# A decoder trunk on one core: the order of one attention unit, with the value products a unit later

## The chip, the core and the metric

The kernel runs on one core of a Trainium2 chip. TensorE (PE, with its weight loads PEld) multiplies matrices into PSUM banks, VectorE (DVE), ScalarE (ACT) and GpSimd (POOL) work on vectors, and SyncE (SP) issues transfers. The engines run side by side and wait for one another by semaphores. Each engine works through its own instructions in the order in which it is given them, so an instruction that waits holds back everything queued behind it on the same engine. The metric is the device time of one execution in microseconds, the median of several.

## The reference

One decoder layer on 2048 positions of width 1024, in float32. What the change touches is the attention: 16 query heads and 2 key/value heads of width 64, in blocks of 128 queries that see their own block and the one before, with a bias by distance and a sink in each head's softmax.

```
u = x * (1 + scale) + shift
[q | k | v | attn_gate | pool_in | pool_gate | merge_a | merge_p] = u @ W_in
logits = (q . k) / 8 + bias, masked to the last 128 positions
probs  = softmax([logits, sink])[..., :-1]
a = (probs @ v) * SiLU(attn_gate) @ W_attn_proj
p = GroupLinear(MultiScaleCausalPool(pool_in)) * pool_scale * SiLU(pool_gate) @ W_pool_proj
x = LayerNorm(alpha * x + ((sigmoid(merge_a) * a + sigmoid(merge_p) * p) @ W_out) * (1 + gate))
```

## The kernel before

A float32 product is made from pieces: an operand x is split into a high part that TensorE takes exactly and a low part, x minus high, and three matmuls (high by high, high by low, low by high) are added up in PSUM. Splitting a tile is so always a copy on one engine (mostly ScalarE) and a subtraction on another (`low`, line 132, mostly VectorE).

The 2048 positions are worked through in two halves. Each half has a ring of gate products (with the products for query tiles 0 and 1 in it, each tile holding the queries of two heads) and then an attention phase, `attention` (line 736). After both come the output products and the layer norm. The large weight products use a block scheme with fewer multiplications; its additions run on GpSimd.

`attention` has one loop, `for n in range(N + 5)` (line 925), over units. A unit n is one query tile j (two heads) and one block of 128 queries; a half has N = 64 of them, eight for each of eight tiles. The loop is a pipeline written out by hand. In one iteration it works on several units:

- S(n): `score_mms` (line 828), four matmuls of queries by keys into a bank `lg` (two buffers).
- the score step on VectorE, one instruction a head: bias added, and the row's bound `nm` reduced, into the tile L; then ScalarE's exponential with the row's sum `sm`. A small ScalarE copy puts the sink into L before.
- for unit n-1, the reciprocal of `sm` (line 937, VectorE), the scaling of the first head's row (ScalarE) and of the second head's (VectorE, called E1 in the prediction).
- T(n-2): `turn_mms` (line 842), four transposes of the scaled weights into the bank `pt` (one buffer); then ScalarE copies the high part `pth` (line 958), and VectorE subtracts for the low part `ptl`. Each of these has one buffer.
- V: `value_mms` (line 849), four matmuls of the values with `pth` and `ptl` into the bank `pv` (one buffer). The values carry their high and low parts side by side, so the result's two halves have to be added: ScalarE copies one half into `o2` (line 946), and VectorE adds it to the other into the output tile `o`, one instruction a head ("the additions").
- `project(n)` (line 873): nine or twelve matmuls of the next query tiles and of the pool branch, which keep TensorE busy while the other engines do the softmax; from unit 60 on `fill_one` (line 912) does the first products of the next phase in their place.

At the unit's end come steps that are due only in some units: `take_q` (line 757) splits a finished query tile (two ScalarE, then two VectorE instructions), `pool_sums` and `pool_diff` (lines 775 and 792) make the pool branch (ScalarE copies, GpSimd sums, one VectorE subtraction), `finish` (line 804) multiplies by gates on GpSimd and queues stores, and weight tiles are fetched and split.

The order on ScalarE, VectorE, TensorE and GpSimd is the order of the text: `act`, `dve`, `pe` and `pool` are wrapped in `Ordered` (line 50), which keeps each engine's instructions as written. Calls through `nc.` are placed by the planner.

Of the kernel before, what the change touches and what calls it, by code (L numbers as in the profile page):

```python
# [12 lines left out]
F32 = mybir.dt.float32  # L13
F32R = mybir.dt.float32r
AF = mybir.ActivationFunctionType
# [4 lines left out]
P = 128  # L20
# [3 lines left out]
CH = 512  # L24
# [35 lines left out]
def kernel(  # L60
# [675 lines left out]
    def attention(ph, s, q0, nxt):  # L736
# [91 lines left out]
        def score_mms(j, b, q, qs):  # L828
            k0 = P if s == 0 and b == 0 else 0
            lg = bank("lg").rearrange("p (h k) -> p h k", h=2)  # L830
            for h in range(2):
                for hl in range(2):
                    mm(
                        lg[:, h, k0:],
                        qs[:, h, q * P : (q + 1) * P],
                        kk[:, j // 4, hl, b * P + k0 : (b + 2) * P],
                        start=hl == 0,
                        stop=hl == 1,
                    )
# [46 lines left out]
        bts = {0: bias_tile(0)}  # L886
        raw_q = {}
        parts, accs, sums = {}, {}, {}
        lgs, exps, Ls, pvs, outs, ags, pgs = {}, {}, {}, {}, {}, {}, {}
        opened = []  # L890
        act.activation(warm, mhalf, AF.Exp)

# [32 lines left out]
        for n in range(N + 5):  # L925
            j, t, b = n // U, n // NB % 2, n % NB
            if n == 0:
                project(n)
            if n < N:
                lgs[n] = score_mms(j, n % U, b, qs[j, t])  # L930
            pt = None
            if n - 2 in Ls:
                L, k0 = Ls.pop(n - 2)
                pt = turn_mms(L, k0)
            if n - 1 in exps:
                sm = exps[n - 1][2]
                dve.reciprocal(sm, sm)
            if n - 3 in pvs:
                pv = pvs.pop(n - 3)
                jj, tt, bb = (n - 3) // U, (n - 3) // NB % 2, (n - 3) % NB  # L940
                if bb == 0:
                    outs[jj, tt] = tp.tile([P, CH], F32, tag="o", bufs=2, name="o")
                if bb == 1:
                    ags[jj, tt] = ld("ag", gates_d["ag"][s, jj, tt])
                o2 = tp.tile([HD, 2, P], F32, tag="o2", bufs=2, name="o2")
                act.copy(o2, pv[HD:])
                for h in range(2):
                    dve.tensor_tensor(
                        outs[jj, tt][h * HD : (h + 1) * HD, bb * P : (bb + 1) * P], pv[0:HD, h, :], o2[:, h, :], ALU.add
                    )  # L950
            if n - 1 in exps:
                E, e0, sm = exps[n - 1]
                act.activation(E[:, 0, e0:256], E[:, 0, e0:256], AF.Copy, scale=sm[:, 0:1])
            if pt is not None:
                h0 = k0 // P
                pth = tp.tile([P, 2, 2, P], F32R, tag="pth", bufs=1, name="pth")
                ptl = tp.tile([P, 2, 2, P], F32R, tag="ptl", bufs=1, name="ptl")
                act.copy(pth[:, h0:], pt[:, h0:])
            if n < N:
                lg, c0 = lgs.pop(n)  # L960
                L = tp.tile([P, 2, 260], F32, tag="L", bufs=3, name="L")
                nm = tp.tile([P, 2], F32, tag="nm", bufs=4, name="nm")
                sm = tp.tile([P, 2], F32, tag="sm", bufs=4, name="sm")
                act.copy(L[:, :, 256], nsink[:, 2 * j : 2 * j + 2])
# [19 lines left out]
                exps[n] = (L, c0, sm)  # L984
            if pt is not None:
                low(dve, ptl[:, h0:], pt[:, h0:], pth[:, h0:])
            if n - 1 in exps:
                E, e0, sm = exps.pop(n - 1)
                dve.tensor_scalar(E[:, 1, e0:256], E[:, 1, e0:256], sm[:, 1:2], None, ALU.mult)
                Ls[n - 1] = (E, e0)  # L990
            if 0 < n < 60:
                project(n)
            elif n >= 60:
                fill_one(n)
            if pt is not None:
                pvs[n - 2] = value_mms((n - 2) // U, (n - 2) % U, k0, pth, ptl)


            for w in range(1, len(order)):
                at = first[2 * w - 2]  # L1000
                if n == at:
                    tiles[w] = fetch(*order[w])
                if n in (at + 1, at + 2) and tiles[w][0] is not None:
                    raw, hi, lo = tiles[w]
                    if n == at + 1:
                        act.copy(by_two(hi), raw)
                    else:
# [12 lines left out]
            for what in puts:  # L1020
                put(pool if n >= 64 else sp, *what)
            puts.clear()
            for at, x, which in ((57, 0, 0), (60, 1, 0), (62, 0, 1), (64, 1, 1)):
                if n == at:
                    early_hi(x, which)
                if n == at + 1:
                    early_lo(x, which)
            if n in (59, 62):
                nxt_group[n // 62].mid()
            if n == 64:  # L1030
                opened[0].append(nxt_group[0].w[:, 0, :])
                act.copy(opened[0][4], opened[0][0])
            for x, at in done.items():
                kind, m, st = x
                if kind == "q":
                    continue
                if n == at + 2:
                    pgs[m, st] = ld("pg", gates_d["pg"][s, m, st])
                if n == at + 3 + (st == 1 and m + 1 < KT):
                    pl = pool_diff(m, sums.pop((m, st)), accs.pop(x))  # L1040
                    finish("p", pin_d[s], m, st, pl, pgs.pop((m, st)))
            for x, at in done.items():
                if x[0] == "mix" and n == at + 1:
                    sums[x[1:]] = pool_sums(*x[1:], accs[x])
            for x in [x for x in outs if n == x[0] * U + x[1] * NB + NB + 2]:
                finish("a", ain_d[s], *x, outs.pop(x), ags.pop(x))

            if n in (26, 42):
                fill_set("T1", n // 42, nxt_store["T1"], sp)
            for start, name in ((57, "B11"), (58, "B21"), (59, "T2"), (61, "B22")):  # L1050
                if n == start:
                    for half in range(2):
                        fill_set(name, half, nxt_store[name], sp)
            if n == 51:
                for q in nxt_group:
                    q.load(ph, False)
# [488 lines left out]
```

## Time and profile before

| | |
|---|---|
| median of 3 runs | 1769.96 us (1766.4 to 1770.78) |
| the profiled execution | 1771.75 us |
| its span, first to last instruction | 1769.9 us |
| mean granted TensorE clock | 0.992 |
| first attention stretch | 427 to about 690 us |
| second attention stretch | about 1030 to 1298 us |

In the rows that follow, a line of the timeline is: start, length, engine, source line, operation, written tile <- read tiles, shapes, count, and in brackets the idle time of that engine before it and what ended it. Nearly every row names line 56, which is the wrapper that keeps the order, so rows are told apart by the tiles. A row of waits is: who waited for whom, total us, times, longest. `pv` is the value bank, `lg` the score bank, `pt` the bank of the turned weights, `mm` a projection bank, `L` the weights of a unit, `sm` their sums.

### The profile page before, as it was taken

To read this page: it belongs to the slowest core of one execution; us is meant where nothing else is said; L and a number is where in the kernel's file an instruction comes from. 1 tells how busy PE (TensorE), PEld (TensorE's weight loads), DVE (VectorE), ACT (ScalarE), POOL (GpSimd) and SP (SyncE) were. 2 spreads that over 40 slices of the span, in tenths; PEclk is the share of its full clock that TensorE was granted. 3 is DMA by queue.
4 is the path that set the end of the run, shared out by engine and by line. 5 is a ranking of instruction groups with operands and counts; after the bars stand their busy time and mean duration, and the time that the engine had idled before them with its cause. 6 is when DMAs were issued, how large, how long until landed. Compare 5 with 4: busy or idle time off the path is not lost. (4 is left out here: it accounts for less than half of the span.)

```text
span 1769.9 us, 24992 instructions
## 1 busy us (share of the span) xinstructions
PE 1701.8 (96%) x8224; PEld 1422.5 (80%) x8224; DVE 1212.4 (68%) x2188; ACT 941.5 (53%) x1983; POOL 803.5 (45%) x624
## 2 busy tenths in 40 slices
PE   6899999999999998999999999999999989999997
PEld 5688888888888887888788888888878767888785
DVE  5977656546777777767745457777867676865777
ACT  4644444436777776444444367777744333423452
POOL 2155444530545567433424224455763663363542
PEclk9999999999999999999999999999999999999998
DMA  9385767853434467687776544454696684699432
GB/s 364 119 287 178 266 215 262 286 130 125 167 135 166 147 230 301 242 276 262 260 273 230 188 162 163 141 178 136 246 355 221 191 261 170 240 322 366 155 143 107
DMA packets 182161, 383.40 MB, mean 217 GB/s; under 512 B 18944, under 2 KB 39440, under 8 KB 182032
## 3 DMA queue, kind: packets, MB, share of 16 engines
q1 hardware_dynamic: 175392, 366.02, 59.1%
q0 software_dynamic: 3552, 11.56, 1.7%
q10 hardware_dynamic: 3088, 4.23, 0.9%
q8 instruction: 65, 1.06, 0.2%
q14 instruction: 64, 0.52, 0.1%
HBM read 245.40 MB, written 139.49 MB: 217 GB/s over the span
## 5 line engine op out<-in xcount | busy, mean ns | idle before, releaser
L56 PE MATMUL mm<-set_B,w_set 128*128 128x512 f32 x3096 | 768.5, 395 | 12.4 <-DVE w_set L133 5.5
L56 PEld LDWEIGHTS mm<-set_B,w_set 128*128 128x128 f32 x3096 | 577.3, 189 | 134.2 <-DVE w_set L133 10.6
L56 PE MATMUL lg<-set_T,w_set 128*128 128x512 f32 x2160 | 523.6, 392 | 17.3 <-DVE w_set L133 9.3
L56 PEld LDWEIGHTS lg<-set_T,w_set 128*128 128x128 f32 x2160 | 404.2, 188 | 110.8 <-DVE w_set L133 14.9
L133 DVE TENSOR_TENSOR w_set<-W,w_set 128x1024 fp32r<-128x1024 f32 x168 | 232.2, 1382 | 205.4 <-ACT w_set L326 195.2
L326 ACT CAST w_set<-W 128x1024 fp32r<-128x1024 f32 x168 | 176.3, 1050 | 266.8 <-PE mm L56 204.9
L56 PE MATMUL mm<-set_T,w_set 128*128 128x512 f32 x1032 | 257.6, 394 | 0.0
L56 PEld LDWEIGHTS mm<-set_T,w_set 128*128 128x128 f32 x1032 | 192.3, 189 | 39.5
L295 POOL TENSOR_TENSOR W<-W,A 128x512 f32<-128x512 f32 x58 | 86.5, 1491 | 237.9 <-DMA A<-in_win_dram 58.2
L304 POOL TENSOR_TENSOR W<-W 128x512 f32<-128x512 f32 x58 | 81.8, 1410 | 189.0 <-DVE w_set L133 178.7
L56 ACT ACTIVATE L<-L,nm 128x257 f32<-128x257 f32 (+1 forms) x256 | 127.1, 498 | 11.0 <-DVE nm L56 5.7
L299 POOL TENSOR_TENSOR W<-W 128x512 f32<-128x512 f32 x58 | 92.0, 1587 | 89.5 <-DVE w_set L133 80.4
L56 DVE TENSOR_TENSOR o<-pv,o 64x128 f32<-64x128 f32 x256 | 72.4, 283 | 81.0 <-ACT o L56 77.9
L56 DVE CUSTOM_DVE_ANT_0 L<-lg,bt,nsink 128x256 f32<-128x256 f32 (+1 forms) x256 | 111.6, 473 | 5.7 <-PE lg L56 1.7
L300 POOL TENSOR_TENSOR W<-W 128x512 f32<-128x512 f32 x58 | 94.6, 1630 | 43.8 <-DMA W<-in_win_dram 27.6
L56 POOL TENSOR_TENSOR p<-nxt,pg 128x512 f32<-128x512 f32 x32 | 41.3, 1292 | 113.5 <-DVE sm L56 113.0
L56 POOL TENSOR_TENSOR nxt<-vb 128x512 f32<-128x512 f32 (+3 forms) x32 | 34.2, 1068 | 122.7 <-ACT vb L56 122.7
L56 DVE TENSOR_TENSOR ptl<-pt,pth 128x512 fp32r<-128x512 f32 (+1 forms) x128 | 85.6, 669 | 1.7 <-ACT pth L56 1.5
L56 ACT COPY o<-pv 64x256 f32<-64x256 f32 x128 | 47.3, 370 | 66.1 <-PE pv L56 65.0
L56 DVE TENSOR_TENSOR k_lo<-spare,k_hi 128x512 fp32r<-128x512 f32 x61 | 61.4, 1009 | 30.0 <-ACT k_hi L56 13.2
L56 ACT ACTIVATE L<-L,sm 128x256 f32<-128x256 f32 (+1 forms) x128 | 64.3, 502 | 31.6 <-DVE sm L56 31.6
L56 PE MATMUL lg<-kk,qs 128*128 128x256 f32 (+1 forms) x512 | 80.3, 279 | 0.0
(217 smaller groups left out, 2347.3 us busy)
## 6 DMA issues: line engine op xcount, KB each, us to landing
W<-in_win_dram SPq DMA_DIRECT2D x48, 512.0 KB, 4.9
w_set<-wmix_d SPq DMA_DIRECT2D x28, 512.0 KB, 4.7
W<-in_win_dram SPq DMA_DIRECT2D x36, 256.0 KB, 3.2
A<-in_win_dram SPq DMA_DIRECT2D x36, 256.0 KB, 4.5
ag_d<-sig SPq DMA_DIRECT2D x32, 256.0 KB, 3.5
pg_d<-sig SPq DMA_DIRECT2D x32, 256.0 KB, 3.5
ma_d<-sig SPq DMA_DIRECT2D x32, 256.0 KB, 4.0
mp_d<-sig SPq DMA_DIRECT2D x32, 256.0 KB, 3.7
```

The costliest lines, as they stand in the source:

```text
L56: return lambda *args, **kw: self.tc.keep_in_program_order(op(*args, **kw))
L133: engine.tensor_tensor(dst, src, as32(hi), ALU.subtract)
L295: e.tensor_tensor(self.w[:, 1, :], self.w[:, 2, :], self.a22, ALU.add)
L299: e.tensor_tensor(x[:, 1, :], x[:, 1, :], x[:, 0, :], ALU.subtract)
L300: e.tensor_tensor(x[:, 2, :], x[:, 0, :], x[:, 2, :], ALU.subtract)
L304: e.tensor_tensor(x[:, 3, :], x[:, 3, :], x[:, 1, :], ALU.subtract)
L326: a.copy(by_two(hi), raw)
```

## The change

In the same loop, the order of an iteration changes and the value products come a unit later, for unit n-3 in place of n-2. What each engine does in iteration n, in order:

| engine | before | after |
|---|---|---|
| TensorE | S(n), T(n-2), projection, V(n-2) | S(n), V(n-3), T(n-2), projection |
| ScalarE | o2(n-3), first head's scaling(n-1), pth(n-2), sink copy(n), exponentials(n) | sink copy(n), first head's scaling(n-1), o2(n-3), pth(n-2), exponentials(n) |
| VectorE | reciprocal(n-1), additions(n-3), score steps(n), ptl(n-2), second head's scaling(n-1) | reciprocal(n-1), score steps(n), ptl(n-2), second head's scaling(n-1), additions(n-3) |

The steps that are due only in some units still follow all this. The tile `o` and the load of the gate `ag` move with the additions. No buffer count changes. The core of the diff:

```diff
             if n < N:
-                lgs[n] = score_mms(j, n % U, b, qs[j, t])
-            pt = None
+                lg, c0 = score_mms(j, n % U, b, qs[j, t])
+            pt = pv = None
+            if n - 3 in turned:
+                pv = value_mms((n - 3) // U, (n - 3) % U, *turned.pop(n - 3))
             if n - 2 in Ls:
                 L, k0 = Ls.pop(n - 2)
-                pt = turn_mms(L, k0)
+                pt, h0 = turn_mms(L, k0), k0 // P
+            if 0 < n < 60:
+                project(n)
+            elif n >= 60:
+                fill_one(n)
+            if n < N:
+                L = tp.tile([P, 2, 260], F32, tag="L", bufs=3, name="L")
...
+                act.copy(L[:, :, 256], nsink[:, 2 * j : 2 * j + 2])
             if n - 1 in exps:
-                sm = exps[n - 1][2]
-                dve.reciprocal(sm, sm)
-            if n - 3 in pvs:
-                pv = pvs.pop(n - 3)
...
+                E, e0, r = exps[n - 1]
+                dve.reciprocal(r, r)
+                act.activation(E[:, 0, e0:256], E[:, 0, e0:256], AF.Copy, scale=r[:, 0:1])
+            if pv is not None:
                 o2 = tp.tile([HD, 2, P], F32, tag="o2", bufs=2, name="o2")
                 act.copy(o2, pv[HD:])
-                for h in range(2):
-                    dve.tensor_tensor(
-                        outs[jj, tt][h * HD : (h + 1) * HD, bb * P : (bb + 1) * P], pv[0:HD, h, :], o2[:, h, :], ALU.add
-                    )
...
             if pt is not None:
                 low(dve, ptl[:, h0:], pt[:, h0:], pth[:, h0:])
+                turned[n - 2] = k0, pth, ptl
             if n - 1 in exps:
-                E, e0, sm = exps.pop(n - 1)
-                dve.tensor_scalar(E[:, 1, e0:256], E[:, 1, e0:256], sm[:, 1:2], None, ALU.mult)
+                E, e0, r = exps.pop(n - 1)
+                dve.tensor_scalar(E[:, 1, e0:256], E[:, 1, e0:256], r[:, 1:2], None, ALU.mult)
                 Ls[n - 1] = (E, e0)
-            if 0 < n < 60:
-                project(n)
-            elif n >= 60:
-                fill_one(n)
-            if pt is not None:
-                pvs[n - 2] = value_mms((n - 2) // U, (n - 2) % U, k0, pth, ptl)
+            if pv is not None:
...
+                for h in range(2):
+                    dve.tensor_tensor(
+                        outs[jj, tt][h * HD : (h + 1) * HD, bb * P : (bb + 1) * P], pv[0:HD, h, :], o2[:, h, :], ALU.add
+                    )
```

More of the change, by code (lines that the diff above doesn't have):

```diff
@@ L888, in attention @@
         parts, accs, sums = {}, {}, {}
-        lgs, exps, Ls, pvs, outs, ags, pgs = {}, {}, {}, {}, {}, {}, {}
+        exps, Ls, turned, outs, ags, pgs = {}, {}, {}, {}, {}, {}
         opened = []
@@ L929, in attention @@
             if n < N:
-                lgs[n] = score_mms(j, n % U, b, qs[j, t])
-            pt = None
+                lg, c0 = score_mms(j, n % U, b, qs[j, t])
+            pt = pv = None
+            if n - 3 in turned:
+                pv = value_mms((n - 3) // U, (n - 3) % U, *turned.pop(n - 3))
             if n - 2 in Ls:
                 L, k0 = Ls.pop(n - 2)
-                pt = turn_mms(L, k0)
-            if n - 1 in exps:
-                sm = exps[n - 1][2]
-                dve.reciprocal(sm, sm)
-            if n - 3 in pvs:
-                pv = pvs.pop(n - 3)
[L940 to L944, printed above, removed]
+                pt, h0 = turn_mms(L, k0), k0 // P
[5 more added lines that the diff above has]
+                L = tp.tile([P, 2, 260], F32, tag="L", bufs=3, name="L")
+                nm = tp.tile([P, 2], F32, tag="nm", bufs=4, name="nm")
+                sm = tp.tile([P, 2], F32, tag="sm", bufs=4, name="sm")
+                act.copy(L[:, :, 256], nsink[:, 2 * j : 2 * j + 2])
+            if n - 1 in exps:
+                E, e0, r = exps[n - 1]
+                dve.reciprocal(r, r)
+                act.activation(E[:, 0, e0:256], E[:, 0, e0:256], AF.Copy, scale=r[:, 0:1])
+            if pv is not None:
                 o2 = tp.tile([HD, 2, P], F32, tag="o2", bufs=2, name="o2")
                 act.copy(o2, pv[HD:])
-                for h in range(2):
-                    dve.tensor_tensor(
-                        outs[jj, tt][h * HD : (h + 1) * HD, bb * P : (bb + 1) * P], pv[0:HD, h, :], o2[:, h, :], ALU.add
-                    )
-            if n - 1 in exps:
-                E, e0, sm = exps[n - 1]
-                act.activation(E[:, 0, e0:256], E[:, 0, e0:256], AF.Copy, scale=sm[:, 0:1])
             if pt is not None:
-                h0 = k0 // P
                 pth = tp.tile([P, 2, 2, P], F32R, tag="pth", bufs=1, name="pth")
@@ L959, in attention @@
             if n < N:
[L960 to L964, printed above, removed]
                 for h in range(2):
@@ L986, in attention @@
                 low(dve, ptl[:, h0:], pt[:, h0:], pth[:, h0:])
+                turned[n - 2] = k0, pth, ptl
             if n - 1 in exps:
-                E, e0, sm = exps.pop(n - 1)
-                dve.tensor_scalar(E[:, 1, e0:256], E[:, 1, e0:256], sm[:, 1:2], None, ALU.mult)
+                E, e0, r = exps.pop(n - 1)
+                dve.tensor_scalar(E[:, 1, e0:256], E[:, 1, e0:256], r[:, 1:2], None, ALU.mult)
                 Ls[n - 1] = (E, e0)
-            if 0 < n < 60:
-                project(n)
-            elif n >= 60:
-                fill_one(n)
-            if pt is not None:
-                pvs[n - 2] = value_mms((n - 2) // U, (n - 2) % U, k0, pth, ptl)
+            if pv is not None:
+                jj, tt, bb = (n - 3) // U, (n - 3) // NB % 2, (n - 3) % NB
+                if bb == 0:
+                    outs[jj, tt] = tp.tile([P, CH], F32, tag="o", bufs=2, name="o")
+                if bb == 1:
+                    ags[jj, tt] = ld("ag", gates_d["ag"][s, jj, tt])
+                for h in range(2):
+                    dve.tensor_tensor(
+                        outs[jj, tt][h * HD : (h + 1) * HD, bb * P : (bb + 1) * P], pv[0:HD, h, :], o2[:, h, :], ALU.add
+                    )
             for w in range(1, len(order)):
```

## The prediction

> **What bounds the kernel now.** I read the page first (engine shares), then the busy time by stretch, then the waits of TensorE's weight loads inside the two attention stretches, then the order of time in two units of the loop.
>
> ```profile
> span 1769.9 us, 24992 instructions
> PE 1701.8 (96%) x8224; PEld 1422.5 (80%) x8224; DVE 1212.4 (68%) x2188; ACT 941.5 (53%) x1983; POOL 803.5 (45%) x624
> ```
>
> The busy time by stretch (PE, PEld, DVE, ACT, POOL, then granted clock, DMA share and GB/s), first and second attention stretch:
>
> ```profile
> 427.00:720.00 293.00, 283.62 (x1570) 243.15 (x1569) 219.26 (x652) 214.86 (x625) 162.40 (x135) 0.99 0.53 188
> ...
> 1010.00:1300.00 290.00, 284.83 (x1603) 245.91 (x1602) 212.79 (x637) 213.66 (x616) 148.47 (x116) 1.00 0.53 184
> ```
>
> TensorE sets the pace (284 of 293 us); VectorE and ScalarE are three quarters full. So only a wait of TensorE costs time. Its waits on the other engines' loop work, in the first and then the second stretch:
>
> ```profile
> PEld pv L56 <- DVE ptl L56: 6.7, 11, 0.7
> ...
> PEld pv L56 <- ACT pth L56: 2.6, 5, 0.9
> ```
>
> ```profile
> PEld pv L56 <- DVE ptl L56: 7.4, 11, 0.7
> PEld pv L56 <- ACT pth L56: 2.2, 4, 0.9
> ```
>
> That is 6.7 + 2.6 + 7.4 + 2.2 = 18.9 us, in 22 units of 128: the value product V waits for the low part ptl of the turned weights. This is all that the change can save. VectorE also waits 39.3 us in the second stretch for the copy o2, ahead of its additions:
>
> ```profile
> DVE o L56 <- ACT o L56: 39.3, 46, 1.6
> ```
>
> but VectorE is not the bound, so that alone is worth nothing. An undisturbed unit with nine projection matmuls, in order of time (start, length):
>
> ```profile
> 1096.19 0.28 PE L56 MATMUL pv<-pth,vv 128*128 128x256 f32 x1
> ...
> 1096.57 0.54 PEld L56 LDWEIGHTS lg<-kk,qs 128*128 128x128 f32 x4
> 1096.69 0.63 PE L56 MATMUL lg<-kk,qs 128*128 128x256 f32 x4
> 1096.88 0.37 ACT L56 COPY o<-pv 64x256 f32<-64x256 f32 x1 [1.44 <-PE pv L56]
> 1097.05 0.46 PEld L56 LDWEIGHTS pt<-ident,L 128*128 128x128 f32 x4
> 1097.16 0.51 ACT L56 ACTIVATE L<-L,sm 128x256 f32<-128x256 f32 x1
> 1097.16 0.60 PE L56 MATMUL pt<-ident,L 128*128 128x128 f32 x4
> 1097.29 0.58 DVE L56 TENSOR_TENSOR o<-pv,o 64x128 f32<-64x128 f32 x2 [1.64 <-ACT o L56]
> 1097.48 1.93 PEld L56 LDWEIGHTS mm<-set_B,w_set 128*128 128x128 f32 x9
> ...
> 1097.79 0.59 ACT L56 CAST pth<-pt 128x512 fp32r<-128x512 f32 x1
> ...
> 1098.50 0.51 ACT L56 ACTIVATE L<-L,nm 128x257 f32<-128x257 f32 x1
> 1098.71 0.68 DVE L56 TENSOR_TENSOR ptl<-pt,pth 128x512 fp32r<-128x512 f32 x1
> 1099.01 0.49 ACT L56 ACTIVATE L<-L,nm 128x257 f32<-128x257 f32 x1
> 1099.32 0.34 DVE L56 TENSOR_SCALAR L<-L,sm 128x256 f32<-128x256 f32 x1
> 1099.45 0.19 PEld L56 LDWEIGHTS pv<-pth,vv 128*128 128x128 f32 x1
> 1099.51 0.56 ACT L56 COPY vb<-mm 128x512 f32<-128x512 f32 x1
> 1099.58 0.68 DVE L56 SCALAR_TENSOR_TENSOR nxt<-nxt,mm 128x512 f32<-128x512 f32 x1
> 1099.68 0.19 PEld L56 LDWEIGHTS pv<-ptl,vv 128*128 128x128 f32 x1
> ...
> 1100.15 0.64 PE L56 MATMUL lg<-kk,qs 128*128 128x256 f32 x4
> ```
>
> Count from the score product S at 1096.69: turn T at 0.47, ptl from 2.02 to 2.70, V's second load (the first that needs ptl) at 2.99, next S at 3.46. The margin is 0.29 us; in a unit with twelve projection matmuls 3 x 1.93/9 = 0.64 more.
>
> **The change, part by part.** No instruction is added or removed; the loop's order is changed on three engines.
>
> TensorE. In steady state V(n-3) and S(n) swap places: ..V,S,T,projection becomes S,V,T,projection. The unit's own length stays 3.46. On VectorE the score steps move ahead of the additions, which frees the score bank earlier; it has two buffers and no wait for it is in the lists, so this is worth 0. On ScalarE the sink copy and the first head's scaling go ahead of o2; o2 is not late by it (below). V now reads pth and ptl made a whole unit earlier, so the 18.9 us of waits on them go. What is late next is the bank: pv has one buffer, and V of a unit may start only when the additions of the unit before have read it. They used to start 0.60 after S; now they are last on VectorE, behind ptl and the scaling of the second head (E1, the TENSOR_SCALAR row).
>
> The new unit worked out from these rows. V's load follows S's by the 0.48 that T's follows it now (1096.57 to 1097.05): 0.36. V's matmuls at 0.48, T 0.50 later (1096.19 to 1096.69): 0.98. pth starts 0.63 after T (1097.16 to 1097.79): 1.61; the copy o2, 0.69 after V (1096.19 to 1096.88), is at 1.17 and out of the way. ptl follows pth by its 0.59 and a handover of 0.03: 2.23. E1 0.61 later: 2.84. The additions 0.26 later: 3.10; with their 0.58 and a handover of 0.05 the bank is free at 3.73. The next V's load wants it at 3.46 + 0.36 = 3.82. So the quiet unit still fits, but with 0.09 us to spare in place of 0.29. ScalarE's exponentials start 0.48 after pth and end their issue at 3.10, where the next ScalarE step now starts at 2.82 (1099.51): 0.28 later.
>
> Now the units that stall, all after a unit that splits a query tile (take_q, two steps on each engine at the unit's end):
>
> ```profile
> 1107.15 1.18 ACT L56 ACTIVATE qs<-mm 64x512 fp32r<-64x512 f32 x2
> ...
> 1108.37 1.39 DVE L56 SCALAR_TENSOR_TENSOR qs<-mm,qs 64x512 fp32r<-64x512 f32 x2 [0.42 <-ACT qs L56]
> ...
> 1108.49 0.63 PE L56 MATMUL lg<-kk,qs 128*128 128x256 f32 x4
> ...
> 1109.77 0.17 DVE L56 RECIPROCAL sm<-sm 128x2 f32<-128x2 f32 x1
> ...
> 1110.03 0.51 ACT L56 ACTIVATE L<-L,sm 128x256 f32<-128x256 f32 x1 [0.98 <-DVE sm L56]
> 1110.57 0.59 ACT L56 CAST pth<-pt 128x512 fp32r<-128x512 f32 x1
> ...
> 1111.40 0.69 DVE L56 TENSOR_TENSOR ptl<-pt,pth 128x512 fp32r<-128x512 f32 x1
> ...
> 1112.14 0.19 PEld L56 LDWEIGHTS pv<-ptl,vv 128*128 128x128 f32 x1 [0.70 <-DVE ptl L56]
> ```
>
> The reciprocal comes r = 1.28 after S. Now: V's load at r + 2.37, wanted at 3.00, so the stall is r - 0.63 (0.65 here). New: first scaling r + 0.26, o2 0.54 later (1110.03 to 1110.57 is that step's spacing), pth 0.27 later (1096.88 to 1097.16) at r + 1.07, ptl r + 1.69, E1 r + 2.30, additions r + 2.56, bank free r + 3.19, wanted at 3.82: the stall is again r - 0.63. The longer chain behind ptl eats all that the later deadline gives. And r itself is 0.28 larger, because take_q stands behind the exponentials. So the stalls are not removed but handed from ptl to the additions, and grow:
>
> (a) 22 stalls, 18.9 us, come back with 0.28 more each: +6; bounds 0, if VectorE's freed time brings r back, and 22 x 0.56. (b) The loop calls take_q 14 times in a stretch and 11 units stall; the other three, with twelve matmuls, have 0.64 more room. I take them to clear it narrowly, and 0.3 each: +2, bounds 0 and 4. (c) Carry. In a stalled unit VectorE now has the additions and any trailing step (the pool difference, 0.68, row 1099.58) between the release of V and the next reciprocal, which so starts about 0.3 + 0.75 = 1.05 after the next S, where 0.2 to 0.3 is usual now. After a nine-matmul unit's limit of 0.63 that is 0.4 of new stall, and a take_q behind it starts half a us later. There are 16 pool differences in a stretch; I take six to lie so, at 0.5: +6, bounds 0 and 12. (d) E1 is now in V's chain, and it is uneven:
>
> ```profile
> L56 DVE TENSOR_SCALAR L<-L,sm x128: 275/346/1468, 430.6 to 1290.6; 128x256 f32<-128x256 f32 x120, 128x128 f32<-128x128 f32 x8
> ```
>
> ```profile
> L56 DVE TENSOR_SCALAR L<-L,sm 128x256 f32<-128x256 f32 x56 | 31.5, 563 | 0.0
> ```
>
> Mean 563 less median 346 is 0.22 us of excess a unit; today it lies behind ptl, where it delays nothing at once. The planned 672 projection matmuls of a stretch, spread over 61 shares of nine or twelve, make 20 units of nine; these can hide 0.09 of it: 40 x 0.13 = +5. Bounds: 0, if the slow ones fall into twelve-matmul units, and 12, if they gather in the short ones.
>
> The Trainium skill ("SBUF — State Buffer", section "Who interferes with whom") says that such a VectorE step and a GpSimd step exclude each other: the later one waits for the other to end. The trace agrees as far as it goes (up to 1.47 us for a 0.35 us step). By that rule E1 would meet GpSimd in 148.47/290 = half of all units and wait half of its 1.3 us steps, an estimated 0.33 a unit; term (d) would be 40 x 0.24 = 10, not 5.
>
> POOL: the products of a finished query tile (finish "a") wait for the additions, which end 2.5 us later; 16 in each stretch. GpSimd is half idle, so this is hidden save at the stretch's end, where the pool difference follows GpSimd's sums closely: +2 in all, bounds 0 and 5. SP: the gate load "ag" is issued later in the unit, past no other SP issue of that unit; TensorE waits for no DMA of the loop in either stretch: 0. At the end of a stretch (units 64 to 66) no S is left, and TensorE's order comes out as before. The one wait there is at the end of the first stretch:
>
> ```profile
> PE mm L56 <- ACT u L377: 4.7, 1, 4.7
> ```
>
> It hangs on ScalarE and VectorE steps behind the last additions, which stay the last of the loop: 0, bounds -4.7, if they come earlier, and +2.
>
> Sum: -18.9 (old waits) + 18.9 (same stalls on the bank) + 6 + 2 + 6 + 5 + 2 = +21 us. The profiled execution took 1771.75 us (span 1769.9), 1.8 above the median 1769.96; the sum is a difference, so I set it on the median: 1791.
>
> **The rivals.** Faster: the bank is free before V wants it in nearly every unit, and the 18.9 us go for good: 1751. This decides if the chain from T to the end of the additions is shorter than worked out, by 0.6 or more, in the late units; for it speak the 39.3 us that VectorE no longer waits for o2, against it that those waits lie ahead of ptl while the new chain goes through pth on ScalarE. One for one: stalls change their name only, (a) to (d) cancel against VectorE's freed waits: 1765 to 1775. Much slower: quiet nine-matmul units lose their 0.09 too (a handover of 0.1 more in the five-step chain gives 40 x 0.1 = 4) and the carry chains from unit to unit at double (c) and (d): 1791 + 4 + 6 + 5 = 1806.
>
> **How the numbers follow.** My sum: 0.6, 1778 (only (a) and (b)) to 1800. Much slower: 0.17, to 1808. One for one: 0.1. Faster: 0.13. The range leaves out the faster case and a few in a hundred above: 1765 to 1808. Within 0.3% is 5.3 us, about what a measurement here can tell from no change. Faster 0.13; same 0.1; slower 0.77. Predicted: 1791.
>
> **What would show it.** Right: in the waits of TensorE's weight loads, "pv <- DVE ptl" and "pv <- ACT pth" gone, and "pv <- DVE o" in their place with 35 to 45 us over both stretches; VectorE's wait for o2 gone, a wait for pth ahead of ptl in its place; E1 at 2.8 after S. Wrong: pv waiting under 20 us in all (the chain is shorter, or take_q lies elsewhere), or pv quiet and the turn pt or the score lg waiting instead; an effect outside the two stretches would be one that I do not see.

## The result, and the profile after

The changed kernel takes 1796.9 us (median of four runs, 1795.04 to 1798.24) against 1770.01 us for the kernel before on the same chip: a ratio of 1.0155, 95% interval 1.0138 to 1.0173, or 27 us slower. The profiled execution took 1798.24 us. The head of its page:

```profile
span 1796.4 us, 24982 instructions
...
PE 1704.6 (95%) x8224; PEld 1424.9 (79%) x8224; DVE 1209.4 (67%) x2188; ACT 933.7 (52%) x1983; POOL 803.0 (45%) x624
```

No engine has more work: TensorE is busy 1704.6 us, 2.8 more than before, and VectorE 3.0 us less. What has grown is the time in which TensorE does nothing: 91.8 us of the span where it was 68.1. The busy time by stretch (length, then PE, PEld, DVE, ACT, POOL, granted clock, DMA share, GB/s); the second window is 30 us wider than the one shown of before, because the stretch now ends later:

```profile
427.00:720.00 293.00, 270.69 (x1507) 232.52 (x1506) 210.91 (x638) 205.59 (x614) 155.28 (x130) 0.99 0.50 175
1010.00:1330.00 320.00, 303.10 (x1676) 260.26 (x1675) 219.61 (x643) 214.16 (x623) 151.84 (x118) 1.00 0.50 175
```

In the first window, of the same length as before, TensorE is busy 270.69 us where it was 283.62, at the same clock. How long the two stretches are can be read from the score product's group: duration in ns (shortest, median, longest), then the start of the first and of the last. First before, then after:

```profile
L56 PE MATMUL lg<-kk,qs x256: 220/281/333, 427.7 to 677.2; 128*128 128x256 f32 x112, 128*128 128x128 f32 x16
L56 PE MATMUL lg<-kk,qs x256: 276/282/286, 1030.8 to 1284.5; 128*128 128x256 f32 x128
```

```profile
L56 PE MATMUL lg<-kk,qs x256: 220/282/333, 429.7 to 689.4; 128*128 128x256 f32 x112, 128*128 128x128 f32 x16
L56 PE MATMUL lg<-kk,qs x256: 277/283/286, 1045.9 to 1309.9; 128*128 128x256 f32 x128
```

Before: 249.5 and 253.7 us. After: 259.7 and 264.0. So 20.5 of the 26.5 us between the two spans arose before the last score product of a stretch; the other 6.0 are taken up below. The waits of TensorE's weight loads, first and second stretch:

```profile
PEld pv L56 <- ACT L L56: 13.1, 12, 2.0
PEld pv L56 <- issue: 6.3, 10, 1.8
...
PEld pv L56 <- ACT qs L56: 1.1, 2, 0.6
PEld pv L56 <- ACT W L56: 1.1, 1, 1.1
```

```profile
PEld pv L56 <- ACT L L56: 14.2, 13, 2.0
PEld pv L56 <- issue: 6.0, 10, 1.8
PEld pv L56 <- ACT W L56: 1.0, 1, 1.0
...
PEld pv L56 <- ACT qs L56: 0.4, 1, 0.4
```

The waits on ptl and pth are gone. The value product waits 13.1 + 6.3 + 1.1 + 1.1 = 21.6 us in the first stretch and as much in the second: 43.2 us where it was 18.9. The names on the right mislead: the ScalarE steps L, qs and W had ended well before, and "issue" is time with no releaser found. The same waits seen from the matmuls, first and second stretch, carry the right name:

```profile
PE pv L56 <- DVE o L56: 16.4, 20, 1.9
PE mm L56 <- ACT u L377: 5.2, 1, 5.2
```

```profile
PE pv L56 <- DVE o L56: 16.8, 22, 1.8
```

42 times the value product waits for the additions, its bank's last reader. VectorE in its turn no longer waits for the copy o2 but for pth (second stretch), and GpSimd, whose gate products of a query tile need the additions, waits 16.4 us for them there where it waited 7.3:

```profile
DVE ptl L56 <- ACT pth L56: 48.5, 64, 1.6
```

```profile
POOL a L56 <- DVE o L56: 16.4, 6, 5.9
```

One late unit in order of time (start, length, in brackets the idle time before and what ended it):

```profile
1125.82 0.64 PE L56 MATMUL lg<-kk,qs 128*128 128x256 f32 x4
...
1125.94 1.39 DVE L56 SCALAR_TENSOR_TENSOR qs<-mm,qs 64x512 fp32r<-64x512 f32 x2 [0.63 <-ACT qs L56]
...
1127.35 0.17 DVE L56 RECIPROCAL sm<-sm 128x2 f32<-128x2 f32 x1
...
1128.40 0.59 ACT L56 CAST pth<-pt 128x512 fp32r<-128x512 f32 x1
...
1129.02 0.69 DVE L56 TENSOR_TENSOR ptl<-pt,pth 128x512 fp32r<-128x512 f32 x1 [0.58 <-ACT pth L56]
...
1129.63 0.34 DVE L56 TENSOR_SCALAR L<-L,sm 128x256 f32<-128x256 f32 x1
...
1129.89 0.57 DVE L56 TENSOR_TENSOR o<-pv,o 64x128 f32<-64x128 f32 x2
...
1130.49 0.69 DVE L56 SCALAR_TENSOR_TENSOR nxt<-nxt,mm 128x512 f32<-128x512 f32 x1
...
1130.58 0.19 PEld L56 LDWEIGHTS pv<-pth,vv 128*128 128x128 f32 x1 [0.88 <-ACT L L56]
...
1131.10 0.16 DVE L56 RECIPROCAL sm<-sm 128x2 f32<-128x2 f32 x1
```

The query tile's two subtractions, the step that split it, end at 1127.33, so the reciprocal comes r = 1.53 after the score product. Then ptl, the second head's scaling E1 and the additions follow one another without a gap; the additions end at 1130.46, and the load of the next value product starts at 1130.58, 0.88 late. The other way to be late, in the same trace: a GpSimd step, the E1 step beside it, and what follows.

```profile
1063.45 2.37 POOL L56 TENSOR_TENSOR w_set<-W,w_set 128x1024 fp32r<-128x1024 f32 x1
...
1063.79 2.17 DVE L56 TENSOR_SCALAR L<-L,sm 128x256 f32<-128x256 f32 x1
...
1065.89 0.57 DVE L56 TENSOR_TENSOR o<-pv,o 64x128 f32<-64x128 f32 x2
...
1066.58 0.19 PEld L56 LDWEIGHTS pv<-pth,vv 128*128 128x128 f32 x1 [1.79 <-issue]
```

Here the unit was on time up to E1. E1 takes 2.17 us where 0.35 is usual and ends 0.14 us after the GpSimd step, and the value product waits 1.79 us, although E1 belongs to another unit's weights. Over the whole run E1's shortest, median and longest are:

```profile
L56 DVE TENSOR_SCALAR L<-L,sm x128: 277/346/2231, 432.6 to 1319.1; 128x256 f32<-128x256 f32 x120, 128x128 f32<-128x128 f32 x8
```

48 of these 128 steps take over 0.5 us ("long" from here on), and each of the 48 ends 0.08 to 0.16 us after the end of a GpSimd step. Read unit by unit in the same trace, the 43.2 us of waits fall on 50 units:

| the wait follows | units | us |
|---|---|---|
| the split of a query tile, E1 not long | 22 | 17.6 |
| the split of a query tile, and a long E1 | 4 | 7.6 |
| a long E1 without a split | 18 | 12.1 |
| the last three units of a stretch, behind its last score product | 6 | 5.9 |

All other units keep their pace. In an undisturbed one with nine projection matmuls E1 starts 2.81 us after the score product, the additions end at 3.64, and the next load of the value product starts at 3.80 without a wait:

```profile
1152.14 0.64 PE L56 MATMUL lg<-kk,qs 128*128 128x256 f32 x4
...
1154.95 0.34 DVE L56 TENSOR_SCALAR L<-L,sm 128x256 f32<-128x256 f32 x1
...
1155.21 0.57 DVE L56 TENSOR_TENSOR o<-pv,o 64x128 f32<-64x128 f32 x2
...
1155.94 0.19 PEld L56 LDWEIGHTS pv<-pth,vv 128*128 128x128 f32 x1
```

### The profile page after: what moved, and what is told of

It is laid out like the page before. It is cut to its first block, busy times and chain, and to the rows that moved or that the text cites. A ratio compares the mean times of both kernels' runs of the same rounds, so it can differ in the third digit from the quotient of the medians.

```text
span 1796.4 us, 24982 instructions
## 1 busy us (share of the span) xinstructions
PE 1704.6 (95%) x8224; PEld 1424.9 (79%) x8224; DVE 1209.4 (67%) x2188; ACT 933.7 (52%) x1983; POOL 803.0 (45%) x624
## 5 line engine op out<-in xcount | busy, mean ns | idle before, releaser
L56 PE MATMUL mm<-set_B,w_set 128*128 128x512 f32 x3096 | 767.7, 395 | 13.8 <-DVE w_set L133 6.5
L56 PEld LDWEIGHTS lg<-set_T,w_set 128*128 128x128 f32 x2160 | 405.7, 189 | 109.3 <-DVE w_set L133 13.6
L304 POOL TENSOR_TENSOR W<-W 128x512 f32<-128x512 f32 x58 | 81.7, 1409 | 189.1 <-DVE w_set L133 175.1
L299 POOL TENSOR_TENSOR W<-W 128x512 f32<-128x512 f32 x58 | 90.4, 1560 | 94.6 <-DVE w_set L133 85.6
L300 POOL TENSOR_TENSOR W<-W 128x512 f32<-128x512 f32 x58 | 91.5, 1578 | 42.7 <-DMA W<-in_win_dram 32.0
L56 PE MATMUL pv<-pth,vv 128*128 128x256 f32 x248 | 68.5, 297 | 33.8 <-DVE o L56 33.2
L56 PEld LDWEIGHTS lg<-kk,qs 128*128 128x128 f32 x512 | 77.9, 189 | 9.9
L56 PEld LDWEIGHTS pv<-pth,vv 128*128 128x128 f32 x248 | 46.9, 189 | 43.5 <-ACT L L56 27.3
```

What stands on the lines that cost most here:

```text
L56: return lambda *args, **kw: self.tc.keep_in_program_order(op(*args, **kw))
L299: e.tensor_tensor(x[:, 1, :], x[:, 1, :], x[:, 0, :], ALU.subtract)
L300: e.tensor_tensor(x[:, 2, :], x[:, 0, :], x[:, 2, :], ALU.subtract)
L304: e.tensor_tensor(x[:, 3, :], x[:, 3, :], x[:, 1, :], ALU.subtract)
```

## The experiments

Each was run beside the kernel before on one chip, so each has a ratio of its own; a difference between two kernels is the difference of their ratios times 1770 us (some 4 us uncertain). "Waits" are those of TensorE's loads for the value product, both stretches together.

| kernel | ratio to before (95%) | us against before | waits, us |
|---|---|---|---|
| after | 1.0155 (1.0138 to 1.0173) | +27.4 | 43.2 |
| 1 additions ahead of E1 | 1.0090 (1.0073 to 1.0106) | +15.9 | 26.2 |
| 2 additions ahead of ptl | 0.9974 (0.9962 to 0.9986) | -4.6 | 6.7 |
| 3 two banks | 1.0078 (1.0057 to 1.0099) | +13.8 | in other places |
| 4 TensorE's order alone | 1.0015 (1.0001 to 1.0029) | +2.7 | 14.8 |
| 5 after, subtractions a unit later | 1.0126 (1.0110 to 1.0142) | +22.3 | 37.2 |
| 6 both 2 and 5 | 0.9964 (0.9951 to 0.9978) | -6.4 | 3.1 |
| 7 before, subtractions a unit later | 1.0003 (0.9990 to 1.0017) | +0.5 | 11.3 |
| 8 after, no subtractions | 1.0039 (1.0026 to 1.0052) | +6.9 | 21.8 |
| 9 before, no subtractions | 0.9933 (0.9912 to 0.9954) | -11.9 | 1.9 |
| 10 after, E1 not held | 1.0104 (1.0089 to 1.0119) | +18.4 | 33.3 |
| 11 both 8 and 10 | 0.9937 (0.9919 to 0.9956) | -11.2 | 5.4 |
| 12 before, E1 not held | 1.0010 (1.0000 to 1.0019) | +1.8 | 18.8 |

### 1: the additions ahead of E1

```diff
             if pt is not None:
                 low(dve, ptl[:, h0:], pt[:, h0:], pth[:, h0:])
                 turned[n - 2] = k0, pth, ptl
-            if n - 1 in exps:
-                ...
-                dve.tensor_scalar(E[:, 1, e0:256], E[:, 1, e0:256], r[:, 1:2], None, ALU.mult)
             if pv is not None:
                 ...
+            if n - 1 in exps:
+                ...
+                dve.tensor_scalar(E[:, 1, e0:256], E[:, 1, e0:256], r[:, 1:2], None, ALU.mult)
```

> The changed kernel with one swap on VectorE: the additions go ahead of the second head's scaling (E1), so that E1 leaves the chain that frees the value bank. Bank theory (the value product waits for the additions to read its one bank, and the stall is the reciprocal's lateness less a limit): the bank is free 0.27 us sooner in each unit and E1's unevenness no longer counts, so the 43 us of waits ahead of pv fall by 10 to 15, and the kernel takes 1782 to 1788. Rival 1 (it is the load or the order on VectorE as a whole): the same work in nearly the same order, 1794 to 1799. Rival 2 (TensorE's order, score before value, costs by itself): 1794 to 1799.

Measured: 11.5 us less than after, as expected. The first stretch shows what is left, and what has come in for it:

```profile
PEld pv L56 <- ACT L L56: 11.3, 14, 2.0
...
PEld pt L56 <- DVE L L56: 2.9, 6, 0.7
```

So E1's place in the chain accounts for a part, and out of the chain it makes the turn T wait, which needs it in the next unit. (The edit also gives the bank back some 0.27 us sooner in every unit, so not all of the 11.5 need be E1's unevenness.)

### 2: the additions in VectorE's gap

```diff
+            if pv is not None:
+                ...  # the additions
             if pt is not None:
                 low(dve, ptl[:, h0:], pt[:, h0:], pth[:, h0:])
                 ...
-            if pv is not None:
-                ...  # the additions
```

> The changed kernel with the additions put between the score steps and the low part ptl on VectorE, where VectorE waits for ScalarE's pth anyway (48.5 us of such waits in the second stretch). Bank theory: the bank is free about 1.8 us after the reciprocal in place of 3.2, so nearly no wait ahead of pv is left; what is late next is ptl and the scaled weights after units with a split query tile, some 4 to 6 us in each stretch. 1758 to 1768, at or below the kernel before. Rival 1: VectorE has as much to do, the waits only change their name, 1785 or more. Rival 2: 1794 to 1799.

Measured: 32 us less than after, and 4.6 us less than before. A late unit (score product at about 1119.1), VectorE and the next load of the value product:

```profile
1120.36 0.15 DVE L56 RECIPROCAL sm<-sm 128x2 f32<-128x2 f32 x1
...
1121.85 0.58 DVE L56 TENSOR_TENSOR o<-pv,o 64x128 f32<-64x128 f32 x2 [0.54 <-ACT o L56]
1122.46 0.69 DVE L56 TENSOR_TENSOR ptl<-pt,pth 128x512 fp32r<-128x512 f32 x1
1123.07 0.42 DVE L56 TENSOR_SCALAR L<-L,sm 128x256 f32<-128x256 f32 x1
...
1123.30 0.19 PEld L56 LDWEIGHTS pv<-pth,vv 128*128 128x128 f32 x1
```

The additions stand in the time in which VectorE would wait for pth. ScalarE's pth, which ptl needs, ends at 1122.36, and ptl starts at 1122.46, so it is at most 0.1 us later than it could be; the bank is free at 1122.43, 0.87 us ahead of the load. With the additions there, the changed order as a whole is a small gain on before.

### 3: a second bank for the value product

```diff
-                pv = value_mms((n - 3) // U, (n - 3) % U, *turned.pop(n - 3))
+                pv = value_mms((n - 3) // U, (n - 3) % U, *turned.pop(n - 3), "lg" if n % 2 and n < 62 else "pv")
```

(`value_mms` takes its bank by that name; every other value product goes into a score bank.)

> The changed kernel, order untouched, but the value products take the bank pv and one of the two score banks in turn, so that each has the additions' whole next unit to be read. Bank theory: the waits of pv on the additions go; ptl and the scaled weights are late next, 5 to 8 us in each stretch: 1763 to 1773. Rival 1 (order and load on VectorE and ScalarE): 1790 to 1799, since no vector instruction moves. Rival 2 (score before value on TensorE): 1794 to 1799.

Measured: 13.6 us less than after, half of what I expected. First stretch:

```profile
PEld lg L56 <- DVE ptl L56: 3.3, 7, 0.5
PEld lg L56 <- DVE nm L56: 2.3, 4, 1.1
PEld pv L56 <- DVE ptl L56: 2.1, 4, 0.5
PEld pt L56 <- DVE L L56: 2.0, 4, 0.7
PEld lg L56 <- ACT pth L56: 1.9, 3, 1.0
```

The wait for the additions is nearly gone (5.1 us in TensorE's matmuls over both stretches, where after has 33.2), and the late units now wait at ptl, pth, the turn and the score bank instead. So for about half of the loss the bank was only the place where TensorE met VectorE's lateness. (One of the two banks is a score bank, so the waits on `nm` may come from the edit itself.)

### 4: TensorE's order alone

After's order on TensorE; ScalarE and VectorE in the order of before, so the additions again come right behind the reciprocal.

```diff
                 dve.reciprocal(r, r)
-                act.activation(E[:, 0, e0:256], E[:, 0, e0:256], AF.Copy, scale=r[:, 0:1])
             if pv is not None:
                 act.copy(o2, pv[HD:])
+                ...  # the additions
+            if n - 1 in exps:
+                act.activation(E[:, 0, e0:256], E[:, 0, e0:256], AF.Copy, scale=r[:, 0:1])
```

> TensorE's order of the changed kernel (score, value of n-3, turn, projection) with ScalarE's and VectorE's order of the kernel before (additions first, ahead of the score steps). Bank theory: the bank is free by 2.2 us into the unit, no wait of pv on the additions; but the score steps wait for the copy o2, which is a us later than before, so the exponentials and the reciprocal come 0.6 us later and the units after a split query tile stall on ptl or the scaled weights, about 10 us in each stretch: 1766 to 1780. Rival 2 (the swap on TensorE is the cost): 1794 or more.

Measured: 24.7 us less than after, 2.7 above before. So the value product's later place costs next to nothing; 24.7 of the 27.4 us belong to the order on VectorE and ScalarE that was changed with it, and experiment 2, which keeps ScalarE's new order, puts them on the additions' place on VectorE.

### 5, 6, 7: the query tile's subtractions a unit later

In the loop, `take_q` leaves its two VectorE steps for the next unit's end, where ScalarE's halves have long been done.

```diff
+            while lows:
+                lows.pop(0)()
             ...
-                qs[x[1:]] = take_q(accs.pop(x))
+                qs[x[1:]] = take_q(accs.pop(x), lows)
```

On after (5):

> The changed kernel with VectorE's half of take_q (two instructions) issued one unit after ScalarE's half, so that the reciprocal behind it no longer waits for ScalarE. Nothing of the change's own order moves. Theory (the stall on the bank is the reciprocal's lateness, and that comes from take_q): the reciprocal comes about 1.0 after the score in place of 1.5 to 2.9, the waits ahead of pv fall from 43 us to 18 to 24, and the ratio to the kernel before is 1.001 to 1.005 (the changed kernel has 1.0155). Rival (the longer chain itself, with the uneven scaling and the pool difference, makes most of the stall): 1.010 to 1.016.

On experiment 2 (6):

> The additions in VectorE's gap ahead of ptl, as in the experiment before, and VectorE's half of take_q a unit later. Theory: both causes are gone, 2 to 4 us of waits are left in both stretches; ratio to the kernel before 0.990 to 0.994. Rival (lateness comes from elsewhere): as with the gap alone, 0.997.

On before (7):

> The kernel before, its order of the unit untouched, with VectorE's half of take_q a unit later. Theory: the 22 stalls on ptl there have the same cause, and the reciprocal's lateness of at most 0.9 falls into units of twelve matmuls, whose limit is about 1.3; 13 to 17 of the 19 us go: ratio 0.990 to 0.993. Rival (the two steps only move, VectorE is as full a unit later): 0.996 to 1.001.

Measured: 5.1 us less than after (5), 1.8 less than experiment 2, with intervals that overlap (6), and nothing against before (7). My theory fell in all three: that VectorE waits for ScalarE's half of the split is not what makes it late, or only a small part of it. The 1.4 us of work stay and make another unit late: of the 37.2 us of waits in 5, 18.1 still fall on units behind the subtractions, where after had 25.2. In 7 the value product's waits fall by 7.6 us without a gain in time; the turn and the score product wait 3.7 us more, and the rest is within what the measurement can tell. Experiment 6 has the lowest ratio of the kernels that compute everything, 0.9964 of before.

### 8, 9: no subtractions at all

```diff
             for h in range(2):
                 a, b = h * HD, (1 - h) * HD
-                dve.scalar_tensor_tensor(qs[b : b + HD, h, :], acc[a : a + HD, :], -0.125, ...)
+                pool.memset(as32(qs[b : b + HD, h, :]), 0.0)
```

> The kernel after, with the low half of each split query tile set to zero by GpSimd instead of worked out by VectorE's two subtractions (so the low part of the queries is left out of the scores; the number of matmuls is the same). VectorE loses 2 x 0.69 us in the unit that splits a tile, the 28 units that the prediction's terms (a) and (b) hang on. Theory: these subtractions are what makes VectorE late, and the late reciprocal is what the bank's stalls come from: most of the 43.2 us of the value product's waits go, the time comes to 0.992 to 1.002 of the kernel before. Rival: the longer chain makes the stalls in any unit with a trailing step (pool differences) or with a second-head scaling held up by GpSimd, and the subtractions are just one cause among several: 1.006 to 1.012, with 25 us or more of the waits left.

> The kernel before with the same edit (the low part of the queries set to zero by GpSimd, VectorE's two subtractions left out). Theory: the 18.9 us of waits of the value product on ptl and pth hang on the same subtractions and go nearly all: 0.989 to 0.993 of the kernel before. Rival: half of the lateness has other causes: 0.994 to 0.998.

Measured: after loses 20.5 us, before 11.9. In before, the value product's waits all but vanish (18.9 to 1.9 us; the turn's grow to 3.9). In after they only halve, to 21.8, which lies between the two expectations. Some 16 us of what is left in after follow a unit whose E1 took 0.95 us or more; the worst one, GpSimd's steps first and then E1:

```profile
1156.90 1.10 POOL L56 MEMSET qs<- 64x512 f32 x2
1157.96 1.29 POOL L56 TENSOR_TENSOR a<-o,ag 128x512 f32<-128x512 f32 x1
1159.21 2.34 POOL L56 TENSOR_TENSOR w_set<-W,w_set 128x1024 fp32r<-128x1024 f32 x1
```

```profile
1158.20 3.50 DVE L56 TENSOR_SCALAR L<-L,sm 128x256 f32<-128x256 f32 x1
```

It ends 0.15 us after the last of two GpSimd steps that follow each other without a gap, and the next value product is 3.06 us late. There is one such wait in each stretch, in units that waited 1.97 and 1.95 us in after. The edit has its own part in them: the zeroing takes GpSimd 1.10 us just ahead of these steps, and E1, with no subtractions in front of it, comes earlier, so that it meets them from the start; the longest E1 of after was 2.23 us. Behind the wait shown the granted clock was also 0.64 from 1162.3 to 1167.0 us, and from its score product to the next that unit took 8.16 us where the one in the first stretch took 6.58.

### 10, 11, 12: E1 in a form that is not held

```diff
-                dve.tensor_scalar(E[:, 1, e0:256], E[:, 1, e0:256], r[:, 1:2], None, ALU.mult)
+                dve.scalar_tensor_tensor(
+                    E[:, 1, e0:256], E[:, 1, e0:256], r[:, 1:2], pt[:, 1]...[:, e0:], ALU.mult, ALU.subtract
+                )
```

> The kernel after with the second head's scaling (E1) written as scale times weight less a column of the turned weights in PSUM, so that it has one operand in SBUF and one in PSUM, like the pool difference that always took 0.69 us. The second head's weights are wrong by it; the work of every engine stays the same. E1 took 0.35 us at best and up to 2.2 us in the kernel after, 13.5 and 12.9 us over its best in the two stretches. Theory: what holds it are GpSimd's steps, the new form is not held, and E1's being held is what makes the half of the bank's stalls that stayed when the query tile's subtractions were left out (21 of 43 us): the time falls by 15 to 24 us, to 1.002 to 1.007 of the kernel before. Rival (the prediction's term (d) as it was sized): 3 to 8 us, 1.011 to 1.014. Second rival: the form is held too, no change.

> The kernel after with both edits: the low half of a split query tile set to zero by GpSimd in place of VectorE's two subtractions, and the second head's scaling with an operand in PSUM (values wrong by both). Theory: late query tile and held scaling are the whole of what makes VectorE late, so hardly a stall of the value product on its bank is left, 5 us or less of 43, and the new order costs nothing by itself: 0.990 to 0.996 of the kernel before, level with the kernel before under the first edit (0.993). Rival: the new order's longer chain stalls on its own: 10 us or more left, 0.998 to 1.003.

> The kernel before with the second head's scaling with an operand in PSUM (values wrong by it). Theory: in the old order this step stands behind ptl, off the value product's chain, so that its being held costs little there: 0.997 to 1.000. Rival: it makes the next unit's reciprocal late in the old order as well: 0.992 to 0.996.

In these kernels the second head's weights come out wrong, by the column that is subtracted; the number and the size of the steps stay. Measured: the new form is never held. Experiment 10:

```profile
L56 DVE SCALAR_TENSOR_TENSOR L<-L,sm,pt x126: 336/472/474, 436.0 to 1310.4; 128x256 f32<-128x256 f32 x119, 128x128 f32<-128x128 f32 x7
```

It is 0.13 us longer at its usual, and its longest is 0.474 where the old form's was 2.231; 68 of the 126 ran beside a GpSimd step. After loses 9.0 us by it, before nothing. Of experiment 11, TensorE's waits by its matmuls in the first and the second stretch:

```profile
PE pv L56 <- DVE o L56: 1.2, 3, 0.8
```

```profile
PE pv L56 <- DVE o L56: 1.4, 4, 0.7
```

With both edits the bank's stalls are all but gone (2.6 us here; 5.4 in the loads, 3.5 of them behind a stretch's last score product), and the new order costs nothing that can be measured: 0.9937, level with 0.9933 for the old order without the subtractions. The old order with both edits was not run; in it E1's new form alone gained nothing. The kernels of the two orders side by side, in us against before:

| | as it is | no subtractions | E1 not held | both |
|---|---|---|---|---|
| order after | +27.4 | +6.9 | +18.4 | -11.2 |
| order before | 0 | -11.9 | +1.8 | not run |

Taken alone the two are worth 20.5 and 9.0 us to after, together 38.6, which is 9 us more than their sum (uncertain by some 6). The trace of after speaks against two causes that hide behind each other: they meet in only 4 units (7.6 us). What the traces show instead are costs of the edits' own, which are gone when both are made. In experiment 8 the units behind a split wait 0.7 us in place of 17.6 where E1 was not long, but the four with both causes still wait 6.1, all of it in the two lumps of 3.06. In experiment 10 the longer form of E1 adds to the waits behind a split: 20.8 us where after has 17.6, for example 1.01 us where the unit shown first has 0.88.

## Why the prediction was right, step by step

It said 1791 and slower; 1796.9 came, inside the likeliest case's own range of 1778 to 1800. The mechanism held; the sizes of the terms held less well than their sum.

**The swap of places.** The waits on ptl and pth went and the bank took their place, in TensorE's loads with 43.2 us, near the top of the 35 to 45 that were named. Experiments 4 and 2 show that the additions' place is what costs: the same value products cost 2.7 us more than before with the additions early, and 4.6 less with them in the gap.

**The unit worked out by hand.** For r = 1.53 the prediction's steps give pth at 2.60, ptl 3.22, E1 3.83, additions 4.09 after the score product, and a stall of 0.90. The trace has 2.58, 3.20, 3.81, 4.07 and 0.88. For the quiet unit they give E1 at 2.84, the end of the additions at 3.68 and a load at 3.82; the trace has 2.81, 3.64 and 3.80.

**Terms (a) and (b), with the old stalls.** 26.9 us were put on the units that split a query tile. In the trace of after 25.2 us of waits follow such a unit (17.6 + 7.6), and r is 1.53 where before's like unit had 1.28, 0.25 more where 0.28 was taken. Without the subtractions 20.5 us go, with the two lumps of that edit among what stays. Right in size; that the subtractions' place mattered, which I came to think afterwards, is refuted by experiments 5 and 7.

**Term (c), the carry.** In the unit shown, the pool difference starts at 1130.49, and the reciprocal behind it at 1131.10. That is 1.83 after its score product, not the 1.05 that the prediction says, because the score product now comes ahead of the stalled value product and is not late with it. But this unit's turn is 0.88 late, so 0.95 of lateness is left that counts. As for the size, 6 us were taken. In experiment 10, where no E1 is held, only 2.5 us of waits remain in the loop without a split; they fall on six units, each behind a pool difference. So the term was too large, as far as such units show it.

**Term (d), E1.** This term was sized at about half: 5 us were taken, and 12.1 us of waits in the loop follow a long E1 without a split, of which the 2.5 us just named stay when E1 is not held. By the time it measured 9.0 (experiment 10, whose new form is 0.13 longer in every unit) and 11.5 (experiment 1, which also gives the bank back sooner). The mean excess was right (13.6 + 13.0 us in 128 units are 0.21 each, where 0.22 was taken); the mistake was to spread it evenly over the nine-matmul units. It comes in lumps of up to 1.9 us, more than the 0.09 + 0.64 us of margin that a unit with twelve matmuls has. The estimate by the rule of the Trainium skill ("SBUF — State Buffer", section "Who interferes with whom") was 10, nearer to what was measured, but by luck: it took 0.33 a unit, where the trace has 0.21, and spread it in the same way. The same section says that a VectorE step with at most one operand in SBUF, outside the modes that take both ports, does not meet GpSimd; experiment 10 agrees, with 126 such steps and none over 0.474 us.

**The sum.** The old waits and (a) to (d) came to 18.9 + 6 + 2 + 6 + 5 = 37.9 us of waits; 43.2 came. That it is so near is partly luck: (d) was some 5 us too small, (c) some 3 too large, (a) and (b) with the old waits 2 too large, and 5.9 us arose behind the last score products, where the prediction put 0. It held that no score product is left there and TensorE's order comes out as before; but the value products there wait for the additions' bank all the same.

**Outside the stretches.** By the score products, 6.0 of the 26.5 us between the two spans lie outside (spans less the stretches: 1266.7 before, 1272.7 after). This is no separate effect, since three units' turns and value products are still to come when the last score product starts: in after 3.1 and 2.7 us of waits for the bank stand behind it, in before none. The value product's later place also puts one more of them there, about 0.5 us in each stretch. The rest of the kernel differs by some us from profile to profile: less those waits, it has 1265.4 to 1273.4 us over the fourteen profiles. The one wait that the prediction named at the end of the first stretch is 0.5 us longer (5.2 for 4.7). GpSimd's term of 2 us was not tried by itself, and is too small to be seen in this.

**The rivals.** "Faster" needed a chain shorter by 0.6; the chain came out as worked out. "Much slower" would have had quiet units stall; the quiet units kept their pace. "One for one" needed (a) to (d) to cancel against the waits that VectorE is rid of; they did not, and even with E1 never held (experiment 10) 18.4 us are left.

## What to carry to other kernels

When a consumer moves back in a pipeline, its inputs' waits go, but its output's buffer is given back later: write down who reads that buffer last, and where in that engine's queue the reader stands. Put the reader into a gap that the engine already has (here the wait for the other engine's half of a split), not behind the whole unit. And keep a step whose length depends on another engine out of the chain that gives a single buffer back: its mean says little, since its peaks decide.

## What the runs showed of the hardware

The same multiplication by a column took 0.35 us with its only tensor operand in SBUF, or up to 2.23 (3.50 in experiment 8) beside GpSimd's steps. In after 48 of 128 took over 0.5 us, and every one of them ended 0.08 to 0.16 us after a GpSimd step. Two GpSimd steps in a row, 1.29 and 2.34 us, held one E1 through both. Written with a second operand in PSUM it took 0.47 us and was never held in 126 cases, 68 of them beside a GpSimd step. And a wait for a PSUM bank is listed twice: under the weight load with the name of an engine that had been done well before, or of none (13.1 us for ScalarE's L in the first stretch), and under the matmul with that of the bank's reader (16.4 us for VectorE's o).
